# A hybrid decoder step on one core: the input projection split into two passes over the tokens

## The chip, the cores and the metric

The program runs on one core of one Trainium2 chip. Its engines are TensorE (PE; its weight loads are PEld), VectorE (DVE), ScalarE (ACT), GpSimd (POOL) and SyncE (SP), which issues the DMAs. Each engine works through its own instructions in a fixed order and waits on semaphores for the others. The metric is the device time of one execution in microseconds (us).

## The reference

One layer is computed for a prompt group of 2048 tokens and a sample group of 8 x 8 tokens, with the same weights, a model width of 1024 and an inner width of 512 for each of two head groups. In shape:

```
h  = rmsnorm(x);  z = h @ w_in          # 1024 -> 512 | 512 | 4 | 4 | 512 | 512
a_x, a_o, a_i, a_f, b_u, b_g = split(z) # mLSTM input, output gate, gates; GLU value, gate
a_c = silu(causal_conv4(a_x))           # q, k from a_c; v from a_x; 4 heads of 128
ha  = sigmoid(a_o) * headnorm(mlstm_chunkwise(q, k, v, a_i, a_f))   # chunks of 128
u   = b_u * sigmoid(b_g)
cb  = silu(layernorm(causal_conv31(u)))
x   = x + concat(ha, cb) @ w_out
x   = x + cross_attention(rmsnorm(x), memory of 256 tokens) @ x_wo
x   = x + convffn(rmsnorm(x));   y = rmsnorm(x)
```

The mLSTM keeps a 128 x 128 state per head, which goes from chunk to chunk; its decays come from a running sum and a running maximum of the gates. All states are outputs too.

## The kernel before

Every float32 matrix is split into a high part in the matmul format float32r and a low part, and a product is made of three matmuls (`mm3`, line 150): high x high, high x low, low x high. `split` (line 292) makes the high part on ScalarE and the low part on VectorE or GpSimd. The small products of the mLSTM and the transposes are plain float32.

Tokens are worked in 8 chunks of 256 (`CH`); chunk 0 also carries the 64 sample tokens, so its matmuls have 320 columns.

*Input projection* (loop after line 590). For each chunk, `input_part` loads two x tiles, normalises them and makes h, transposed and split, in the tile `ha` or `hb`. Then four parts multiply it by four 512-column pieces of w_in, each held in SBUF as 8 split tiles (32 in all, pool `wp1`): `ogate_part` (weights `wo_`, result to DRAM as `to`), `ax_part` (weights `wa`, the mLSTM's input, to DRAM as `ax`), and `glu_part` (weights `wgt` and `wbv`, result u to DRAM). `gates_part` and `gates_tm_part` make the 8 gate columns with the small weights `wg`. After chunks 3 and 7 `decays` turns the gates of 8 mLSTM tiles into decay factors: a chain of small products in PSUM bank C (`tri`, `av`, `cmo`, `last`, `Mx`), with doubling maximum steps on VectorE between them. The chunk's transposes use banks B and C.

*Depthwise convolution of width 31* (`CONV_BLOCKS`, `conv_block`). It runs over blocks of 1, 2, 2, 2 and 1 chunks, and over the sample group. For each of four channel groups one tap starts the sum in PSUM bank G, most taps are VectorE instructions `psG<-ue,vc,psG`, and the third number of a block, `g` = 10, says how many taps ScalarE multiplies (`cprod`) and GpSimd sums (`cside`) instead. `cvo` is the sum of both; layer norm and swish follow.

*mLSTM loop* (from line 1229). `conv_part` reads `ax` back from DRAM (`axe`) and makes the four-tap convolution `acc`; `qkv_part` makes q and k, `pre_part` the decay matrix `dm`, the decayed q `qi`, v and the weighted k, `recur_part` the recurrence on the state `stt_t`, `head_tail` and `head_out` the head norm and the output gate; the result goes to DRAM as `cat`. Between these, `steps` moves two side programs on: the sample group's mLSTM, and `memory_kv`, the projection of the memory tokens (tiles `hm`). `out_part(t)` reads tile t of `cat` (`ct` is its split form), multiplies it by w_out in banks D and F and adds x: VectorE's `xt<-xt,psD` and `xt<-xt,psF`.

The source gives priorities: the program builder lists each engine's instructions with a timeline of its own and puts, of those that are ready there, the one that comes first in the source. So an engine's order is fixed before the run, and pieces of source that stand apart are interleaved.

Of the kernel before, what the change touches and what calls it, by code (L numbers as in the profile page):

```python
# [9 lines left out]
F32 = mybir.dt.float32  # L10
# [9 lines left out]
P = 128  # L20
# [18 lines left out]
FOLD_AT = 1  # L39
# [54 lines left out]
def trunk_kernel(ctx: ExitStack, tc: tile.TileContext, i: dict, o: list):  # L94
# [67 lines left out]
    xtp = phs.enter_context(tc.tile_pool(name="x1", bufs=2, reuse_waits="tile"))  # L162
# [141 lines left out]
    ax_d = [dram(f"ax{c}", [P, H, CH]) for c in range(NCH)]  # L304
# [11 lines left out]
    wp1 = wa1.enter_context(tc.tile_pool(name="wp1", bufs=32, side="right", reuse_waits="tile"))  # L316
# [44 lines left out]
    def ogate_part(ch, xts, h, n):  # L361
        pts = [mmps() for _ in range(H)]
        if ch == 0:
            for k in range(KT):
                for c in range(H):
                    gemm_k(pts[c], wo_, c * P, h, n, k)
        for c, pt in enumerate(pts):
            if ch:
                gemm_fm(pt, wo_, c * P, h, n)
            tg = ut.tile([P, CH + S], F32, name="tg", tag="tg")  # L370
            act(tg[:, :n], pt[:, :n], AF.Tanh, scale=0.5)
            ts(tg[:, :n], tg[:, :n], 1.0, ALU.add, hnh[:, c:c + 1], ALU.mult)
            for j, (_, nt) in enumerate(xts):
                SY.dma_start(to_d[2 * ch + j if nt == P else NT][:, c, :], tg[:, j * P:j * P + nt])
    def ax_part(ch, xts, h, n):
        for c in range(H):
            pt = mmps()
            gemm_fm(pt, wa, c * P, h, n)
            ax = ut.tile([P, CH + S], F32, name="ax", tag="hu")
            A.copy(ax[:, :CH], pt[:, :CH])  # L380
            SY.dma_start(ax_d[ch][:, c, :], ax[:, :CH])
            if ch == 0:
                A.copy(axs[:, c, :, 3:], pt[:, CH:n].rearrange("p (b t) -> p b t", b=NB))
# [29 lines left out]
    def glu_part(ch, xts, h, n):  # L413
        for c in range(H):
            pg = mmps()
            gemm_fm(pg, wgt, c * P, h, n)
# [130 lines left out]
    def input_part(ch):  # L547
# [6 lines left out]
        return ch, xts, h, CH + (S if ch == 0 else 0)  # L554
# [15 lines left out]
    ts(lnh, vc1[:, o0:o0 + 12], 0.5, ALU.mult)  # L570
    hnh = lnh[:, 8:12]

    wa = load_in(0)
    wgt = load_in(1032 + DA)
    wbv = load_in(1032)
    raws.close()
# [1291 lines left out]
```

## Time and profile before

| | |
|---|---|
| median of 3 runs | 2974.38 us (2971.86 to 2977.52) |
| profiled execution | 2972.23 us, its span 2970.5 us |
| busy in the span | PE 2805.6, PEld 2480.1, DVE 2192.5, ACT 1524.4, POOL 1065.5 us |
| mean granted TensorE clock | 0.969 |
| DMA | 445.63 MB, 150 GB/s on the mean |

Matmuls are pipelined, so the duration of one is longer than the step from one to the next, and a busy PE is not PE at its peak. The change touches what lies before the attention, the first 931 us of the span. A timeline row gives the start, the duration, the engine, the line, the operation, the result and its operands, and, in brackets, how long the engine had been idle and on whom it waited.

### The profile page before, as it was taken

What the parts mean: (1) busy time and instruction counts of PE and PEld (TensorE: products, weight loads), DVE (VectorE), ACT (ScalarE), POOL (GpSimd) and SP (SyncE); (2) the same over time, 40 slices, a digit from 0 to 9 for tenths busy, and PEclk for the clock granted to TensorE, in tenths of its full rate; (3) what the DMA queues carried; (4) which work ended last, traced back from release to release, by engine and by line L of the source; (5) the groups of instructions that cost most, each with busy time, mean ns of one, the idle gap of its engine ahead of it and who ended that gap; (6) DMA issues with size and microseconds to landing.
All of it is one profiled execution on the core that took longest, in us unless ns stands there. A gap on an engine that the chain in (4) does not pass through costs nothing.

```text
span 2970.5 us, 49324 instructions
## 1 busy us (share of the span) xinstructions
PE 2805.6 (94%) x17924; PEld 2480.1 (83%) x17924; DVE 2192.5 (74%) x4066; ACT 1524.4 (51%) x3075; POOL 1065.5 (36%) x1248
## 2 busy tenths in 40 slices
PE   7997997889999799899899999999999999999998
PEld 6996997668887688666588988999989999899987
DVE  3478798986534788745598889877797768877776
ACT  4465665765533665512464446655466545544433
POOL 2235555642210532633433325333253222522222
PEclk9998998979999899999899999999999999999999
DMA  8221223544346422656855555655465545544432
GB/s 193 56 72 50 69 77 124 177 127 158 135 167 218 154 78 96 215 206 228 269 170 163 168 169 195 190 162 161 143 222 160 156 135 164 184 130 133 131 118 75
DMA packets 316571, 445.63 MB, mean 150 GB/s; under 512 B 36605, under 2 KB 219363, under 8 KB 316320
## 3 DMA queue, kind: packets, MB, share of 16 engines
q1 hardware_dynamic: 316328, 442.49, 46.4%
q8 instruction: 141, 2.31, 0.3%
q14 instruction: 102, 0.84, 0.1%
HBM read 348.62 MB, written 94.15 MB: 149 GB/s over the span
## 4 chain that ended last, share of the span: by engine, by line
PE 74%; DVE 13%; DMA 7%; issue 2%; ACT 2%; POOL 1%; SPq 1%; DVEq 0%; POOLq 0%; ACTq 0%
PE psA L148 23%; PE psD L148 14%; PE psF L148 14%; PE psE L148 9%; PE psG L148 8%; DVE psG L122 2%; DMA raw<-in_f_wup 2%; DVE wt L125 2%; PE psC L145 1%; PE psB L145 1%; DVE raw L125 1%; PE psB L148 1%; DVE u L125 1%; DVE acc L122 1%; DMA raw<-in_w_in 1%
## 5 line engine op out<-in xcount | busy, mean ns | idle before, releaser
L294 ACT CAST wt<-raw 128x512 fp32r<-128x512 f32 x888 | 539.5, 620 | 520.5 <-PE psA L148 152.9
L125 DVE TENSOR_TENSOR wt<-raw,wt 128x512 fp32r<-128x512 f32 x666 | 514.5, 788 | 85.3 <-ACT wt L294 81.7
L125 POOL TENSOR_TENSOR wt<-raw,wt 128x512 fp32r<-128x512 f32 x222 | 319.8, 1444 | 671.1 <-ACT wt L294 552.1
L148 PE MATMUL psA<-R,wt 128*128 128x256 f32 (+1 forms) x2448 | 335.4, 287 | 4.6 <-DVE R L122 1.6
L148 PEld LDWEIGHTS psA<-R,wt 128*128 128x128 f32 x2448 | 315.1, 191 | 8.5 <-DVE u L125 1.9
L122 DVE SCALAR_TENSOR_TENSOR psG<-ue,vc,psG 128x512 f32<-128x512 f32 (+2 forms) x488 | 282.5, 579 | 31.3 <-ACT psG L117 22.0
L125 POOL TENSOR_TENSOR cside<-cside,cprod 128x512 f32<-128x512 f32 (+2 forms) x208 | 208.8, 1004 | 140.5 <-ACT cprod L117 86.8
L148 PE MATMUL psA<-wt,ht 128*128 128x512 f32 (+1 forms) x768 | 191.0, 395 | 0.0
L148 PE MATMUL psD<-R,wt 128*128 128x256 f32 (+1 forms) x1248 | 176.6, 286 | 6.9 <-DVE R L125 3.1
L148 PE MATMUL psF<-R,wt 128*128 128x256 f32 (+1 forms) x1248 | 178.2, 287 | 4.3 <-DVE R L122 1.7
L148 PE MATMUL psE<-R,wt 128*128 128x256 f32 (+1 forms) x1224 | 174.4, 287 | 6.2 <-DVE R L125 3.2
L148 PE MATMUL psG<-R,wt 128*128 128x256 f32 (+1 forms) x1224 | 174.7, 287 | 1.9 <-DVE R L122 1.4
L148 PEld LDWEIGHTS psD<-R,wt 128*128 128x128 f32 x1248 | 162.2, 189 | 10.5 <-DVE R L125 4.2
L148 PEld LDWEIGHTS psA<-wt,ht 128*128 128x128 f32 (+1 forms) x768 | 140.6, 185 | 35.0 <-DVE u L125 0.3
L148 PEld LDWEIGHTS psE<-R,wt 128*128 128x128 f32 x1224 | 159.9, 190 | 9.6 <-DVE R L125 4.4
L148 PEld LDWEIGHTS psF<-R,wt 128*128 128x128 f32 x1248 | 162.5, 190 | 6.4 <-DVE u L125 2.4
L148 PEld LDWEIGHTS psG<-R,wt 128*128 128x128 f32 x1224 | 159.8, 190 | 3.1 <-DVE R L122 1.6
L122 DVE SCALAR_TENSOR_TENSOR y<-fe,vc,y 128x512 f32<-128x512 f32 x176 | 130.4, 778 | 14.3 <-ACT y L117 14.3
L117 ACT ACTIVATE cprod<-ue,vc 128x512 f32<-128x512 f32 (+2 forms) x208 | 121.1, 596 | 36.4 <-POOL cside L125 32.6
L148 PE MATMUL psA<-wf,l 128*128 128x512 f32 x516 | 130.9, 401 | 9.0 <-DVE u L125 5.8
L125 POOL TENSOR_TENSOR y<-y,u 128x256 f32<-128x256 f32 x110 | 96.9, 889 | 109.1 <-DVE u L125 90.8
L148 PEld LDWEIGHTS psA<-wf,l 128*128 128x128 f32 x516 | 96.6, 191 | 36.8 <-issue 13.2
(605 smaller groups left out, 6077.4 us busy)
## 6 DMA issues: line engine op xcount, KB each, us to landing
raw<-sum SPq DMA_DIRECT2D x132, 512.0 KB
raw<-in_f_wup SPq DMA_DIRECT2D x110, 512.0 KB
raw<-in_f_wdown SPq DMA_DIRECT2D x88, 512.0 KB
xt<-x SPq DMA_DIRECT2D x48, 512.0 KB
sum<-raw SPq DMA_DIRECT2D x44, 512.0 KB
raw<-in_f_wup SPq DMA_DIRECT2D x66, 256.0 KB
xt<-in_x_prompt SPq DMA_DIRECT2D x32, 512.0 KB
x<-xt SPq DMA_DIRECT2D x32, 512.0 KB
```

Of the source, the lines that this page charges most:

```text
L117: A.activation(out, in_, func, bias=bias, scale=scale)
L122: V.scalar_tensor_tensor(out=out, in0=in0, scalar=s, in1=in1, op0=op0, op1=op1)
L125: (eng or V).tensor_tensor(out=out, in0=a, in1=b, op=op)
L145: T.transpose(out, in_, ident[:n, :n])
L148: T.matmul(out, lhsT, rhs, start=start, stop=stop)
L294: A.copy(hi, src)
```

## The change

The input projection is done in two passes. The first pass makes the gates and the GLU of all chunks, with 16 weight tiles in place of 32, and stores h, split, in DRAM (`h_d`, two stores for a chunk). The weights of the mLSTM's input and of the output gate are loaded while it runs (`load_late`), half of them, and the rest behind it. In the mLSTM loop `rest_part` takes the place of `conv_part`: it loads h of a chunk from DRAM in 8 tiles (a ring of 10), multiplies it by `wa` and by `wo_` in banks D and F, makes the four-tap convolution from the first and the output gate from the second. The buffer `ax` in DRAM goes.

Three more edits go with it. Of the convolution blocks only the first two and the sample's stand ahead of the loop, the others in its iterations 1, 3 and 5 (`CONV_AT`), and ScalarE and GpSimd take 12 taps, not 10. `decays` is called after the next chunk's `input_part`. The side programs move on from iteration 7 only, and the output projections, which were spread over the loop from its third iteration, come in its last iteration and behind it.

```diff
-CONV_BLOCKS = [(0, 1, 10), (1, 2, 10), (3, 2, 10), (5, 2, 10), (7, 1, 10)]
+CONV_BLOCKS = [(0, 1, 12), (1, 2, 12), (3, 2, 12), (5, 2, 12), (7, 1, 12)]
+W2_EARLY = 4
+H2_BUFS = 10
+CONV_AT = {1: 2, 3: 3, 5: 4}
...
-    xtp = phs.enter_context(tc.tile_pool(name="x1", bufs=2, reuse_waits="tile"))
+    xtp = xw = ctx.enter_context(tc.tile_pool(name="xw", bufs=6, side="right", reuse_waits="tile"))
...
-    ax_d = [dram(f"ax{c}", [P, H, CH]) for c in range(NCH)]
+    h_d = [dram(f"h{c}", [P, KT, 2, CH + (0 if c else S)]) for c in range(NCH)]
...
-    wp1 = wa1.enter_context(tc.tile_pool(name="wp1", bufs=32, side="right", reuse_waits="tile"))
+    wp2 = wa2.enter_context(tc.tile_pool(name="wp2", bufs=KT + W2_EARLY, side="right", reuse_waits="tile"))
+    wp1 = wa1.enter_context(tc.tile_pool(name="wp1", bufs=2 * KT, side="right", reuse_waits="tile"))
...
+    def load_late(pool, c0, k):
+        raw = xw.tile([P, 2, 512], F32, name="raw", tag="xt")
+        SY.dma_start(raw, w_in[k * P:(k + 2) * P, c0:c0 + DA].rearrange("(z p) c -> p z c", p=P))
+        out = []
+        for z in range(2):
+            w = pool.tile([P, 2, 512], F32R, name="wt", tag="wt")
+            split(w[:, 0], w[:, 1], raw[:, z], eng=(V, G)[z])
+            out.append([w])
+        return out
...
+        n = CH + (S if ch == 0 else 0)
+        for z in range(2):
+            SY.dma_start(h_d[ch][:, :, z], f(h[:, z, :, :n]))
...
     for ch in range(NCH):
-        order = (ogate_part, ax_part, gates_part, None, glu_part, gates_tm_part)
+        cur_ = cur
+        gates_part(*cur)
         if ch:
-            order = (gates_part, glu_part, gates_tm_part, None, ogate_part, ax_part)
...
+            glu_part(*cur)
+            gates_tm_part(*cur)
+        if ch + 1 < NCH:
+            cur = input_part(ch + 1)
         if ch == 0:
+            glu_part(*cur_)
+            gates_tm_part(*cur_)
             fold_qk()
-        cur = nxt
+        elif len(late) > (KT - W2_EARLY) // 2:
+            late_part(wp2)
+        if 2 * ch + 2 in (GB, NT):
+            decays(2 * ch + 2 - GB)
...
-    def conv_part(ch):
+    def rest_part(ch):
+        n = CH + (S if ch == 0 else 0)
+        hs = []
+        for k in range(KT):
+            hk = h2p.tile([P, 2, CH + S], F32R, name="h2", tag="h2")
+            SY.dma_start(f(hk[:, :, :n]), h_d[ch][:, k])
+            hs.append(hk)
+        def gemm(wts, c):
+            pt = mmps()
+            for k in range(KT):
+                w, m = wts[k][0], slice(c * P, c * P + P)
+                mm3(pt[:, :n], (w[:, 0, m], w[:, 1, m]), (hs[k][:, 0, :n], hs[k][:, 1, :n]), k == 0, k == KT - 1)
+            return pt
         t = m1.tile([P, H, 3 + CH], F32, name="axe", tag="axe")
-        SY.dma_start(t[:, :, 3:], ax_d[ch])
...
+        for c in range(H):
+            pt = gemm(wa, c)
+            A.copy(t[:, c, 3:], pt[:, :CH])
...
         conv4(acc, lambda c, j: t[:, c, j:j + CH])
         st_[ch] = acc
+        for c in range(H):
+            pt = gemm(wo_, c)
+            tg = ut2.tile([P, CH + S], F32, name="tg", tag="tg")
+            act(tg[:, :n], pt[:, :n], AF.Tanh, scale=0.5)
+            ts(tg[:, :n], tg[:, :n], 1.0, ALU.add, hnh[:, c:c + 1], ALU.mult)
+            for j in range(2):
+                SY.dma_start(to_d[2 * ch + j][:, c, :], tg[:, j * P:j * P + P])
...
     for ch in range(NCH + 2):
         if ch < NCH:
             qkv_part(ch)
         if ch + 1 < NCH:
-            conv_part(ch + 1)
+            rest_part(ch + 1)
+        if ch == NCH - 1:
+            wa2.close()
+            wpo0 = out_pool("wpo0", 0, WO_FIRST)
+            next(fold)
+            wout = load_out(wpo0, 0, WO_FIRST)
...
-            if ch > 2:
-                out_part(2 * ch - 6 + j)
...
+            if ch == NCH + 1:
+                for _ in range(2):
+                    out_part(outs.pop(0))
...
+        if ch in CONV_AT:
+            conv_block(*CONV_BLOCKS[CONV_AT[ch]])
+    while outs:
+        out_part(outs.pop(0))
+        steps(0)
```

Three places show how the order moves. The line numbers of the helpers differ by 3 between the programs. The first is TensorE at the first decay chain, at the end of chunk 3. Before (`hb,wt` is chunk 3's projection, `ha` chunk 4's, `ident,cvo` a transpose of the convolution):

```order
L145 MATMUL psC<-ident,av 32x128
L148 MATMUL psD<-hb,wt 128x256 x5
L148 MATMUL psF<-hb,wt 128x256 x24
L145 MATMUL psC<-ident,cmo 128x32
L148 MATMUL psC<-Fs,last 128x32
L148 MATMUL psC<-Mx,last 128x32
L145 MATMUL psE<-ident,cvo 128x128
L145 MATMUL psC<-ident,Mx 32x128
L145 MATMUL psC<-ident,xt 128x128 x2
```

Now, the same chain (its later products follow in the same manner):

```order
L151 MATMUL psC<-wk,tri 128x32
L148 MATMUL psB<-ident,xt 128x128 x2
L151 MATMUL psA<-ha,wg 8x256
L151 MATMUL psA<-ha,wg 16x256
L151 MATMUL psA<-ha,wg 8x256
L151 MATMUL psA<-ha,wt 128x256 x5
L151 MATMUL psD<-ha,wt 128x256 x5
L151 MATMUL psF<-ha,wt 128x256 x5
L148 MATMUL psC<-ident,av 32x128
L151 MATMUL psA<-ha,wt 128x256
```

Before, four products of the chain follow each other and chunk 4's transposes stand behind them; now chunk 4's projection lies between them.

The second is TensorE at the start of the mLSTM loop. Before (`acc,wqk` makes q and k of chunk 0, `stt_t,qi` is the first product of the recurrence):

```order
L148 MATMUL psF<-hb,wt 128x256 x24
L148 MATMUL psA<-acc,wqk 128x256 x4
L148 MATMUL psC<-wk,tri 128x32
L145 MATMUL psE<-ident,cvo 128x128
L145 MATMUL psC<-ident,av 32x128
L148 MATMUL psA<-wqkv,axe 128x128 x4
L148 MATMUL psA<-qk,acc 128x128 x4
L145 MATMUL psA<-ident,acc 128x128 x4
L148 MATMUL psB<-stt_t,qi 128x129
```

Now, some rows behind the first product of the recurrence (`h_...` are tiles of h read back from DRAM):

```order
L148 MATMUL psA<-ident,acc 128x128 x3
L151 MATMUL psA<-wqkv,axe 128x128 x3
L148 MATMUL psE<-ident,cvo 128x128
L151 MATMUL psA<-wqkv,axe 128x128
L151 MATMUL psD<-h_4686,wt 128x256 x3
L148 MATMUL psC<-ident,Mx 32x128
L151 MATMUL psD<-h_4688,wt 128x256 x3
L151 MATMUL psD<-h_4690,wt 128x256 x3
L151 MATMUL psB<-vv,dm 128x129
L151 MATMUL psF<-h_4686,wt 128x256
```

Before, the loop's first chunk has only its own small products; now deferred projection products lie between them and the second decay chain's.

The third is VectorE in a later chunk of the mLSTM loop. Before (`stt_t` is the state's update, `acc` the four-tap convolution):

```order
L122 SCALAR_TENSOR_TENSOR stt_t<-stt_t,ex,psC 128x129
L122 SCALAR_TENSOR_TENSOR acc<-axe,vc_383,acc 128x256 x3
L122 SCALAR_TENSOR_TENSOR acc<-th,acc 128x512 x2
L125 TENSOR_TENSOR xt<-xt,psD 128x512
L125 TENSOR_TENSOR to<-to,psA 128x512
L122 SCALAR_TENSOR_TENSOR stt_t<-stt_t,ex,psC 128x129 x2
L122 SCALAR_TENSOR_TENSOR dm<-mr,av,cap 128x128 x4
L125 TENSOR_TENSOR qi<-qi,qk 128x512
L125 TENSOR_TENSOR xt<-xt,psF 128x512
```

Now:

```order
L125 SCALAR_TENSOR_TENSOR psG<-ue,vc_394,psG 128x512
L714 RECIPROCAL hw<-hw 128x8
L125 SCALAR_TENSOR_TENSOR psG<-ue,vc_394,psG 128x512 x2
L125 SCALAR_TENSOR_TENSOR stt_t<-stt_t,ex,psC 128x129
L125 SCALAR_TENSOR_TENSOR psG<-ue,vc_394,psG 128x512
L125 SCALAR_TENSOR_TENSOR acc<-axe,vc_388,acc 128x256
L125 SCALAR_TENSOR_TENSOR psG<-ue,vc_394,psG 128x512
L125 SCALAR_TENSOR_TENSOR acc<-axe,vc_388,acc 128x256 x3
```

Before, the additions of the output projection stand between the mLSTM's operations; now taps of the long convolution do.

## Rows read from the trace of the kernel before

**Rows 1.** Stages: window, length, busy (instructions) PE, PEld, DVE, ACT, POOL, clock, DMA share, GB/s

```profile
0.00:100.00 100.00, 77.93 (x467) 72.31 (x468) 38.57 (x83) 42.93 (x90) 22.14 (x36) 0.95 0.68 159
100.00:250.00 150.00, 147.45 (x1224) 144.31 (x1223) 103.04 (x262) 90.15 (x205) 66.22 (x100) 1.00 0.21 61
250.00:290.00 40.00, 21.13 (x152) 19.02 (x151) 37.46 (x69) 18.11 (x32) 25.64 (x31) 0.74 0.13 39
290.00:490.00 200.00, 199.40 (x1665) 196.94 (x1662) 164.34 (x292) 125.42 (x253) 97.45 (x113) 1.00 0.24 75
490.00:690.00 200.00, 160.57 (x794) 125.20 (x795) 179.85 (x417) 137.48 (x337) 110.92 (x129) 0.80 0.50 159
690.00:931.00 241.00, 236.10 (x1294) 199.35 (x1291) 104.35 (x220) 96.08 (x270) 34.88 (x47) 1.00 0.42 146
```

**Rows 2.** Three tiles: ns min/median/max, first to last start in us, forms

```profile
L122 DVE SCALAR_TENSOR_TENSOR psG<-ue,vc,psG x488: 270/490/757, 82.9 to 693.6; 128x512 f32<-128x512 f32 x80, 128x256 f32<-128x256 f32 x54, 128x64 f32<-128x64 f32 x29
L125 DVE TENSOR_TENSOR xt<-xt,psD x17: 678/686/689, 690.5 to 952.3; 128x512 f32<-128x512 f32 x16, 64x512 f32<-64x512 f32 x1
L148 PE MATMUL psA<-wt,mT x42: 387/389/501, 931.3 to 967.8; 128*128 128x512 f32 x42
```

**Rows 3.** Timeline of PE at the first decay chain, rows with a wait

```profile
266.28 0.31 PE L145 MATMUL psC<-ident,cmo 32*128 32x32 f32 x1 [8.51 <-DVE cmo L125]
267.04 0.64 PE L148 MATMUL psC<-Fs,last 128*128 128x32 f32 x2 [0.45 <-DVE Mx L526]
...
271.63 0.47 PE L145 MATMUL psE<-ident,cvo 128*128 128x128 f32 x1 [3.52 <-DVE cvo L125]
277.18 0.40 PE L145 MATMUL psC<-ident,Mx 128*32 128x128 f32 x1 [5.08 <-POOL Mx L125]
```

**Rows 4.** Timeline of PE at the start of the mLSTM loop, two waits

```profile
507.37 0.80 PE L148 MATMUL psB<-stt_t,qi 128*128 128x129 f32 x2 [9.87 <-DVE qi L125]
...
515.42 2.08 PE L148 MATMUL psA<-wqkv,axe 128*128 128x128 f32 x8 [2.77 <-DVE dm L125]
```

**Rows 5.** Waits of DVE at 490 to 700, the longest: us, times, longest

```profile
DVE stt_t L122 <- PE psC L148: 8.4, 4, 3.7
```

**Rows 6.** Paces of PE: two pieces of the chain, two timeline rows (start, us)

```profile
117.21 2.88 PE psD L148 x24
...
904.01 5.52 PE psD L148 x24
...
716.14 0.39 PE L148 MATMUL psB<-stt_t,qi 128*128 128x129 f32 x2
716.36 0.39 PE L148 MATMUL psB<-vv,dm 128*128 128x129 f32 x2
```

**Rows 7.** Groups by form at 0 to 940: busy us, mean ns, idle before

```profile
L122 DVE SCALAR_TENSOR_TENSOR psG<-ue,vc,psG 128x512 f32<-128x512 f32 x240 | 179.7, 749 | 7.8 <-ACT psG L117 3.9 <-DMA ue<-u 0.6
L122 DVE SCALAR_TENSOR_TENSOR psG<-ue,vc,psG 128x256 f32<-128x256 f32 x160 | 77.5, 484 | 15.9 <-ACT psG L117 12.9
L117 ACT ACTIVATE cprod<-ue,vc 128x512 f32<-128x512 f32 x108 | 76.5, 720 | 22.8 <-POOL cside L125 20.8 <-DMA ue<-u 1.7
L125 POOL TENSOR_TENSOR cside<-cside,cprod 128x512 f32<-128x512 f32 x108 | 142.9, 1323 | 63.3 <-ACT cprod L117 52.0 <-DVE psG L122 5.8
```

**Rows 8.** The decay matrix's mask at 430 to 700, then at 700 to 930

```profile
L122 DVE SCALAR_TENSOR_TENSOR dm<-mr,av,cap 128x128 f32<-128x128 f32 x32 | 14.2, 497 | 0.2 <-PE psB L148 0.2
...
L122 DVE SCALAR_TENSOR_TENSOR dm<-mr,av,cap 128x128 f32<-128x128 f32 x32 | 9.1, 346 | 7.4 <-PE psB L148 7.3
```

**Rows 9.** DMA issues of weights at 0 to 950

```profile
raw<-in_w_in SPq DMA_DIRECT2D x32, 256.0 KB
...
raw<-in_w_out SPq DMA_DIRECT2D x16, 256.0 KB
raw<-in_x_wk SPq DMA_DIRECT2D x16, 256.0 KB
```

**Rows 10.** The costliest group of projection products at 0 to 940

```profile
L148 PE MATMUL psA<-hb,wt 128*128 128x256 f32 x768 | 99.1, 285 | 0.5 <-ACT tg L117 0.5
```

More of the change, by code (lines that the diff above doesn't have):

```diff
@@ L413, in glu_part @@
     def glu_part(ch, xts, h, n):
-        for c in range(H):
-            pg = mmps()
-            gemm_fm(pg, wgt, c * P, h, n)
+        if ch == 0:
+            pgs = [mmps() for _ in range(H)]
+            for k in range(KT):
+                for c in range(H):
+                    gemm_k(pgs[c], wgt, c * P, h, n, k)
+        for c in range(H):
+            if ch == 0:
+                pg = pgs[c]
+            else:
+                pg = mmps()
+                gemm_fm(pg, wgt, c * P, h, n)
             tg = ut.tile([P, CH + S], F32, name="tg", tag="tg")
@@ L578, in trunk_kernel, with late_part @@
     first_loads()
+    wa, wo_ = [], []
+    late = [(wl, c0, k) for wl, c0 in ((wa, 0), (wo_, DA)) for k in range(0, KT, 2)]
+    def late_part(pool):
+        wl, c0, k = late.pop(0)
+        wl.extend(load_late(pool, c0, k))
     for ch in range(NCH):
[L580 removed]
+        cur_ = cur
+        gates_part(*cur)
         if ch:
[L582 to L589 removed]
+            glu_part(*cur)
+            gates_tm_part(*cur)
+        if ch + 1 < NCH:
+            cur = input_part(ch + 1)
         if ch == 0:
+            glu_part(*cur_)
+            gates_tm_part(*cur_)
             fold_qk()
[L592 removed]
+        elif len(late) > (KT - W2_EARLY) // 2:
+            late_part(wp2)
+        if 2 * ch + 2 in (GB, NT):
+            decays(2 * ch + 2 - GB)
     wa1.close()
@@ L1184, in conv_part @@
         st_[ch] = acc
+        for c in range(H):
+            pt = gemm(wo_, c)
[4 more added lines that the diff above has]
+                SY.dma_start(to_d[2 * ch + j][:, c, :], tg[:, j * P:j * P + P])
+            if ch == 0:
+                SY.dma_start(to_d[NT][:, c, :], tg[:, CH:n])
     mrs = {}
@@ L1227, in steps @@
             next(fold, None)
-    wpo0 = out_pool("wpo0", 0, WO_FIRST)
-    conv_part(0)
-    next(fold)
-    wout = load_out(wpo0, 0, WO_FIRST)
+    rest_part(0)
+    outs = list(range(NT - 2))
     for ch in range(NCH + 2):
@@ L1240, in trunk_kernel @@
                 recur_part(ch - 1, j)
+            if ch >= NCH - 1:
                 steps(0)
@@ L1262, in trunk_kernel @@
             head_tail(m2, nds[ch - 1], P, 2, ex[:, 0, 2 * ch - 2:2 * ch])
+        if ch in CONV_AT:
[3 more added lines that the diff above has]
+        steps(0)
+    for _ in side:
+        pass
+    ahead = [out_load(t) for t in (NT, NT - 2)]
+    out_part(NT, ahead[0])
     for _ in side:
```

70 lines of the change are left out of this document (20 added, 50 removed).

## The prediction, made before the run

> **What bounds the kernel now.** I read the table by stages first, then the instructions that mark the stages' ends, then the waits inside them. The stages [rows 1]: to 490 us the input projection, with the depthwise convolution beside it; 490 to 690 the mLSTM loop with the rest of the convolution and the memory projection; 690 to 931 the output projection beside the rest of the mLSTM. The reader is to see that the limit changes. From 100 to 250 and from 290 to 490 TensorE is full (147.5 of 150, 199.4 of 200 us) and VectorE has room (103.0 and 164.3, or 82% in the second). From 490 to 690 it is turned round: VectorE is busy 179.9 of 200 us. From 690 to 931 TensorE is full again and VectorE is busy 104.4 of 241 us. The markers are the first convolution tap at 82.9, the first addition of an output projection at 690.5 and the first product of the attention's value factors at 931.3 [rows 2]. What comes after that last marker is the same work in the same order in both programs, so I forecast when it starts and carry the difference to the end.
>
> Between these stages TensorE stands still for reasons of order. At 250 to 290 it is busy 21.1 of 40 us: the decay chain on VectorE must come through, and TensorE's next projection work stands behind the chain's small products; it waits 8.5, 0.5, 3.5 and 5.1 us, 17.6 together [rows 3]. At the mLSTM's start it waits 9.9 and 2.8 us, with nothing else in its queue that could run [rows 4]. In the VectorE-bound stage the longest sum of named waits of VectorE is 8.4 us [rows 5]: it is its own work that fills it.
>
> **The change part by part.** Paces: 24 products of 256 columns take 2.88 us, 0.12 each; 24 of 512 columns 5.52 us, 0.23 each; a float32 product of 128 columns 0.22 (716.14 to 716.36) [rows 6].
>
> Start. Each weight matrix has 8 tiles of 256 KB; four of them (32 issues [rows 9]) are loaded before the loop now, two then. Chunk 0 first ran the output gate and the mLSTM input, 2 x 4 x 24 products of 320 columns, at 0.12 x 320/256 = 0.15 each 28.8 us, before it came to the GLU. Those leave, so the first tap comes about 26 us sooner, at 57 (the loads set a floor: 159 GB/s went through in the first 100 us [rows 1], and 4.2 MB fewer have to).
>
> TensorE. No product is added or removed. What it needs ahead of the output projections becomes 2688 x 0.12 + 384 x 0.15 + 128 gate products x 0.12 = 396; 192 of the memory projection x 0.23 = 44; 336 float32 products x 0.22 and 32 of twice the width x 0.44 = 88; and about 500 transposes at 0.11, with the sample group some 70: 600 us, an estimate from the order's counts and the paces. The output projections, 768 products x 0.23 = 177 us, now stand alone behind it, where before the rest of the mLSTM lay beside them. The stalls of [rows 3] go, because the decay products now lie between projection products; those of [rows 4] go, because chunk 0's and 1's deferred products lie there.
>
> VectorE. Up to 690 us it was busy 38.6 + 103.0 + 37.5 + 164.3 + 179.9 = 523.3 us [rows 1]. Of the 104.4 us of the next stage, 30 residual additions at 0.686 (20.6) [rows 2] and 6 operand splits of twice their width (at most 2 x 0.686 each, 8) stay with the output projections; the other 76 now come ahead of them. Two taps per tile go to ScalarE and GpSimd: 12 tiles x 2 x 0.749 + 8 x 2 x 0.484 = 25.7 us less [rows 7]. The masks of the decay matrix took 0.497 us while GpSimd summed taps and 0.346 later [rows 8]; 32 of them now lie beside taps, 4.8, with the convolution of four taps 6 us more. Sum: 523.3 + 76 - 25.7 + 6 = 580, of which about 20 fall before the first tap (half of the first 100 us). 560 us remain. A rule of the Trainium skill bears on this (page "SBUF — State Buffer", section "SBUF: two separate sides"): VectorE and GpSimd hold a shared port exclusively, VectorE when it has two SBUF inputs. [Rows 8] agree in direction; by the rule every such operation pays, and at the row's 0.15 for the 32 masks and 36 four-tap steps that is 10 us in place of 6. It speaks against moving taps to GpSimd, and changes the sum by 4.
>
> What hides the rest. GpSimd gets 24 x 1.323 and 16 x about 0.8, 44 us more; ScalarE 24 x 0.72 and 16 x 0.5, 25 us more [rows 7]; in 490 to 690 they were busy 55% and 69% [rows 1], so nothing is charged. If this cover fails, it is the rival below. The rows h go to DRAM (17 MB) and come back (17 MB, 64 issues on SP's queue), the 8.4 MB of the old intermediate go. The DMA share was 0.24 at 290 to 490 and 0.50 at 490 to 690 [rows 1]; 17 MB over 280 us are 61 GB/s beside 75. Not shown by the trace is how TensorE meets h's return: eight of ten buffers are held until the last product group of a chunk, and eight tiles at 159 GB/s take 13 us. I bound this by 0 (ten buffers and mLSTM products between) and 7 x 10 = 70 us of TensorE time, and take 0, since TensorE has 17% of room in the sum below.
>
> The sum. With a share e of VectorE the first output addition is at 57 + 560/e, and the marker of 931 comes 177 - 3 = 174 us later. e was 0.82 where TensorE was full (290 to 490) and 0.90 where VectorE bound (490 to 690). Both must now run together, so I take 0.84, nearer the lower: 57 + 667 = 724, + 174 = 898, which is 33 us before 931. The profiled execution took 2972.2 us (span 2970.5), 2.2 below the median of the runs; 2972 - 33 = 2939, say 2940. TensorE then works 600 of 707 us from 17 on, 85%. No change is at e = 0.80 (560/0.80 = 700).
>
> **The rivals.** Better overlap: at e = 0.88 the marker is at 867, 64 us sooner, 2908. For it: 290 to 490 has TensorE at 99.7% with VectorE at 82%. Against it: there was no recurrence in it.
>
> The tail eats it: no change. The memory projection, w_out and the sample group's state ran beside the mLSTM before; now they start only when the last deferred rows are done. 48 weight tiles of 256 KB ([rows 9]; the value weights have as many as the key weights), states and stores are about 21 MB; at 159 GB/s 132 us, against the 91 x 0.954/0.84 = 103 us of VectorE work that I count there (estimated from the order and the mean durations). That loses 29 of the 33 us: 2968. Against it: 159 GB/s took only half of the DMA engines' time at 490 to 690 [rows 1].
>
> Two banks: slower. The deferred products have two PSUM banks (D and F) in place of four, each emptied by ScalarE, which now has more taps in front. A group lasts 2.88 us, so a copy that comes over 2.9 us late stops TensorE, and with it the recurrence that VectorE waits for. Up to no change TensorE may stand still 757 - 600 - 17 = 140 us, 2.2 us for each of 64 groups: a copy 5 us late, seven products of 0.72 [rows 7]. At 3 us a group it starts the output projections at 809 and the marker is at 983, 52 us later: 3024. With four banks TensorE waited 0.5 us in the costliest projection group [rows 10], which speaks against it; ScalarE's 69% for it. A rule of the Trainium skill (page "Perfetto Trace Analysis", section "Matmul Optimizations") asks for all eight banks to be used; no run here shows two at this pace.
>
> That rows are not deferred, or the loop not filled, is excluded by the order.
>
> **How the numbers follow.** About 0.2%, 6 us, is what can be told from no change; that is e from 0.79 to 0.81. Forecast, e 0.82 to 0.87: 0.45. Better overlap: 0.13. Tail: 0.17, of which 0.07 within 6 us and 0.10 still faster. Slower by banks, late h tiles or a stiff order (e under 0.79): 0.25. Faster 0.68, same 0.07, slower 0.25. The range goes from e = 0.90 (marker at 853, 78 sooner, 2894) to e = 0.77 (958, 27 later, 2999): 2895 to 3000.
>
> **What would show it.** First tap near 57; no TensorE wait of over 3 us at the two decay chains; in the loop both engines above 80%, the granted clock near 1.00 where it was 0.80; first output addition near 724; then 5.5 us per product group of 24 without waits; first product of the value factors near 898. Wrong would be waits of TensorE on ScalarE's copies from banks D and F, on h tiles, or a stretch between the last deferred product and the first output projection of over 130 us.

## The result, and the profile after

The changed kernel takes 3011.89 us (median of 4 runs, 3008.20 to 3012.39), the kernel before in the same session 2975.61: ratio 1.0121, 95% interval 1.0103 to 1.0138. It is slower by 36 us, where 33 faster was forecast. The profiled execution took 3008.2 us (span 3006.2).

The stages after, with the columns of [rows 1]: start, first pass, loop with the deferred products, the stretch behind the last of them, output projections up to the first value-factor product.

```profile
0.00:100.00 100.00, 52.37 (x281) 42.97 (x282) 31.50 (x68) 32.13 (x66) 19.59 (x34) 0.83 0.73 185
100.00:343.00 243.00, 213.04 (x1635) 200.37 (x1634) 182.75 (x410) 169.45 (x357) 147.51 (x190) 0.94 0.38 122
343.00:649.00 306.00, 283.07 (x2221) 274.43 (x2221) 277.18 (x535) 212.14 (x545) 145.15 (x180) 0.98 0.36 111
649.00:794.50 145.50, 132.79 (x691) 103.67 (x691) 87.24 (x230) 89.45 (x229) 69.62 (x94) 0.88 0.64 201
794.50:965.50 171.00, 169.29 (x765) 136.84 (x763) 35.84 (x55) 18.95 (x30) 20.13 (x9) 1.00 0.40 136
```

The markers of [rows 2] after:

```profile
L125 DVE SCALAR_TENSOR_TENSOR psG<-ue,vc,psG x448: 267/490/824, 70.6 to 695.9; 128x512 f32<-128x512 f32 x72, 128x256 f32<-128x256 f32 x48, 128x64 f32<-128x64 f32 x30
...
L128 DVE TENSOR_TENSOR xt<-xt,psD x24: 674/689/690, 794.5 to 1486.7; 128x512 f32<-128x512 f32 x23, 64x512 f32<-64x512 f32 x1
...
L151 PE MATMUL psA<-wt,mT x42: 387/389/775, 965.5 to 1003.5; 128*128 128x512 f32 x42
```

The last marker moved from 931.3 to 965.5: 34 of the 36 us are lost ahead of it. In the first 100 us TensorE worked 52.4 us, against 77.9 before. The first pass has it at 88%, the loop at 93% with VectorE at 91%; behind the last deferred product VectorE falls to 60%.

The mean granted clock of the first 100 us was 0.83, against 0.95 before. What took the start is seen on three engines. The timeline of TensorE, two rows with their wait:

```profile
85.89 5.23 PE L151 MATMUL psD<-ha,wt 128*128 128x320 f32 x24 [11.09 <-ACT tg L120]
...
97.78 3.78 PE L151 MATMUL psF<-ha,wt 128*128 128x320 f32 x24 [2.88 <-ACT tg L120]
```

The timeline of ScalarE at the tanh that TensorE waits for:

```profile
85.40 0.44 ACT L120 ACTIVATE tg<-psD 128x320 f32<-128x320 f32 x1 [5.52 <-DMA out<-ot]
97.30 0.44 ACT L120 ACTIVATE tg<-psF 128x320 f32<-128x320 f32 x1 [5.70 <-DMA out<-ot]
```

The issues of SyncE's queue just before:

```profile
74.53 1.26 SPq L557 DMA_DIRECT2D h<-hb  x2
75.84 4.02 SPq L435 DMA_DIRECT2D out<-ot  x1
```

The tanh's tile `tg` and the small tile `ot` (the sample's convolution state, stored from chunk 0's GLU) share one tag with two buffers: a ring, whose buffers the tiles take in turn. The store of `ot` was issued right behind two h stores of 1024 KB; until it landed, the tanh had no buffer, the tanh held the PSUM bank, and TensorE stood. To 120 us ScalarE waited 16.1 us for `out<-ot`; before, when the GLU came third and no h was stored, 4.1 us to 200 us.

The decay chain, which answers to [rows 3], on TensorE's timeline after (rows with a wait at 240 to 246):

```profile
241.38 0.69 PE L148 MATMUL psB<-ident,xt 128*128 128x128 f32 x2 [4.19 <-DVE hb L125]
243.80 0.39 PE L148 MATMUL psC<-ident,gT 16*128 16x16 f32 x2 [1.52 <-DVE cmo L545]
245.42 0.66 PE L148 MATMUL psC<-ident,xt 128*128 128x128 f32 x2 [1.23 <-DVE gall L128]
```

The waits for the chain's own results fell from 14.0 us (the 17.6 of [rows 3] hold 3.5 for the convolution's `cvo`) to 1.5; instead TensorE waits beside it for the input of the next chunk (`hb`), 4.2 us at the longest. And TensorE's waits at 343 to 694, which answer to [rows 4]: total, times, longest.

```profile
PE psC L151 <- DVE stt_t L125: 11.8, 6, 6.5
PE psD L151 <- DMA h<-h: 5.4, 5, 2.3
...
PE psD L151 <- ACT axe L1211: 1.9, 2, 1.0
...
PE psF L151 <- DMA h<-h: 1.6, 2, 1.1
```

### The profile page after: what moved, and what is told of

It is laid out like the page before. It is cut to its first block, busy times and chain, and to the rows that moved or that the text cites. A ratio compares the mean times of both kernels' runs of the same rounds, so it can differ in the third digit from the quotient of the medians.

```text
span 3006.2 us, 49437 instructions
## 1 busy us (share of the span) xinstructions
PE 2815.6 (94%) x17924; PEld 2483.7 (83%) x17924; DVE 2179.5 (72%) x4022; ACT 1536.3 (51%) x3115; POOL 1115.3 (37%) x1299
## 4 chain that ended last, share of the span: by engine, by line
PE 70%; DVE 14%; DMA 8%; issue 3%; ACT 2%; POOL 2%; SPq 1%; DVEq 0%; POOLq 0%; ACTq 0%
PE psA L151 20%; PE psD L151 15%; PE psF L151 14%; PE psE L151 9%; PE psG L151 9%; DVE psG L125 3%; DMA raw<-in_f_wup 2%; DVE wt L128 2%; DMA raw<-in_w_in 1%; PE psB L148 1%; PE psC L148 1%; DMA h<-h 1%; DVE acc L125 1%; DVE raw L128 1%; DVE dm L125 1%
## 5 line engine op out<-in xcount | busy, mean ns | idle before, releaser
L128 POOL TENSOR_TENSOR cside<-cside,cprod 128x512 f32<-128x512 f32 (+2 forms) x248 | 251.5, 1015 | 137.5 <-ACT cprod L120 94.4
L125 DVE SCALAR_TENSOR_TENSOR psG<-ue,vc,psG 128x512 f32<-128x512 f32 (+2 forms) x448 | 256.9, 573 | 13.3 <-ACT psG L120 5.6
L120 ACT ACTIVATE cprod<-ue,vc 128x512 f32<-128x512 f32 (+2 forms) x248 | 146.3, 603 | 32.0 <-POOL cside L128 30.9
```

The costliest lines, as they stand in the source:

```text
L120: A.activation(out, in_, func, bias=bias, scale=scale)
L125: V.scalar_tensor_tensor(out=out, in0=in0, scalar=s, in1=in1, op0=op0, op1=op1)
L128: (eng or V).tensor_tensor(out=out, in0=a, in1=b, op=op)
```

## The experiments

All but the first two rows were timed in five rounds beside the kernel before. Medians are compared; the ratio is to the kernel before, with its 95% interval. Kernels of different sessions meet in these comparisons, and the median of the kernel before went from 2972.9 to 2975.6 us between sessions, so differences under 3 us say nothing. "Marker" is the first value-factor product, "busy" TensorE's busy time up to it, by the same view of each profiled execution, "idle" the difference.

| kernel | us | ratio | marker | busy | idle |
|---|---|---|---|---|---|
| before | 2975.6 | 1 | 931.3 | 842.6 | 88.7 |
| after | 3011.9 | 1.0121 (1.0103 to 1.0138) | 965.5 | 850.6 | 114.9 |
| own_ot | 2979.2 | 1.0019 (1.0007 to 1.0030) | 935.6 | 845.4 | 90.2 |
| h_act | 3003.9 | 1.0092 (1.0077 to 1.0108) | 964.5 | 852.9 | 111.6 |
| h_not_stored | 3002.6 | 1.0089 (1.0074 to 1.0104) | 964.3 | 856.8 | 107.5 |
| close_early | 3021.6 | 1.0152 (1.0136 to 1.0167) | 974.1 | 853.1 | 121.0 |
| before_ot | 2964.6 | 0.9968 (0.9958 to 0.9978) | 920.0 | 838.5 | 81.5 |
| h_act_ot | 2994.1 | 1.0056 (1.0036 to 1.0076) | 950.4 | 852.9 | 97.5 |
| mem_first | 3019.0 | 1.0150 (1.0131 to 1.0170) | 979.3 | 874.0 | 105.3 |
| taps10_ot | 2978.9 | 1.0011 (1.0000 to 1.0021) | 933.1 | 850.4 | 82.7 |
| wout_v | 2979.1 | 1.0013 (1.0002 to 1.0024) | 934.6 | 848.0 | 86.6 |
| mem1_after | 2957.2 | 0.9945 (0.9928 to 0.9962) | 914.4 | 824.2 | 90.2 |
| mem1_before | 2941.4 | 0.9888 (0.9871 to 0.9905) | 896.9 | 807.0 | 89.9 |
| before_decays_ot | 2955.9 | 0.9938 (0.9920 to 0.9955) | 917.6 | 845.2 | 72.4 |
| before_best | 2959.7 | 0.9952 (0.9940 to 0.9964) | 919.3 | 846.0 | 73.3 |
| own_rings | 2983.2 | 1.0036 (1.0024 to 1.0048) | 943.9 | 852.0 | 91.9 |
| hp_input | 2985.6 | 1.0045 (1.0033 to 1.0057) | 944.9 | 851.9 | 93.0 |
| nost_ot | 2981.3 | 1.0032 (1.0020 to 1.0045) | 936.8 | 850.9 | 85.9 |
| pe_first | 2987.5 | 1.0046 (1.0028 to 1.0063) | 951.4 | 868.7 | 82.7 |
| pe_loop | 3005.7 | 1.0104 (1.0088 to 1.0121) | 961.0 | 871.4 | 89.6 |

**The start.** Four kernels from the changed one: the ring, the queue, the stores, and (against them) the tail.

```
own_ot:        -  ot = ut.tile([S, P], F32, name="ot", tag="tg")
               +  ot = ut.tile([S, P], F32, name="ot", tag="ot")
h_act:         -  SY.dma_start(h_d[ch][:, :, z], ...)
               +  A.dma_start(h_d[ch][:, :, z], ...)
h_not_stored:  +  if ch == 0:            # around the stores; rest_part reads h_d[0]
close_early:   -  if ch == NCH - 1: wa2.close() ...   steps from ch >= NCH - 1
               +  if ch == NCH - 2: wa2.close() ...   steps from ch >= NCH - 2
```

own_ot. 

> The tile ot (rows of the sample's convolution state) gets buffers of its own and no longer takes turns with the tanh's tile tg. Theory 'ring': ScalarE's tanh waited 16.1 us for the stores of ot before 120 us and 6.6 us later, and PE 11.1 + 2.9 us for that tanh: these waits go, 8 to 15 us off 3011.9. Rival: ScalarE then waits for the late weights or x instead and the time stays within 4 us.

h_act. 

> The h stores are issued from ScalarE's queue and no longer from SyncE's; nothing else changes. Theory 'start' in the form 'order in the queue': weights, x tiles and the stores of ot no longer stand behind 2 x 1280 and 2 x 1024 KB; first convolution tap nearer the forecast 57 us than the 70.6 seen, PE idle in 50 to 100 us 33 -> about 15 us, 10 to 25 us off 3011.9. Rival 'bytes, not order': the transfers share the same engines and take as long from either queue: within 5 us of 3011.9, first tap at 70 again.

h_not_stored. 

> Only chunk 0's h is stored, and the deferred products of all eight chunks read that one back, so the gates of chunks 1 to 7 are computed from wrong rows; the reading, the products and everything behind them stay. Theory 'start': the h stores stand in the one transfer queue ahead of weights, x tiles and small stores. But chunk 0's own store (2 x 1280 KB, issued at 25.0 us) stays here, so only what chunk 1's store (issued at 74.5) and the later ones cost can go: the wait of the tanh for the store of ot and the late x of chunk 1, 10 to 25 us off the changed kernel's 3011.9, most of it before 130 us. Rival 'late weights': the start is lost to ScalarE's casts of the late weights, whoever is in the queue: under 5 us. Neither expects the tail behind 650 us to move.

close_early. 

> The pool of the deferred weights is closed one step of the loop earlier (right behind the products of the last chunk), and the memory projection and the sample group start there, at step 6 and no longer at step 7. Theory 'tail': these two are exposed behind 650 us because nothing else is left to run beside them; one step of the loop earlier they find some 40 us of work beside them, 20 to 40 us off 3011.9, all of it between the last deferred product (648.7) and the first product with value factors (965.5). Rival 'full loop': VectorE is about 90% busy in the loop, so what is moved there lengthens it by as much: within 8 us of 3011.9.

The ring was the larger cost by far: own_ot takes 33 us off, more than twice what was expected. The stall had pushed all of the first pass back: without it its last product comes at 296.5 and no longer at 339.9. The stages of own_ot, columns as above:

```profile
0.00:100.00 100.00, 76.79 (x482) 68.17 (x483) 36.39 (x82) 43.02 (x89) 23.86 (x41) 0.93 0.72 194
100.00:299.00 199.00, 179.43 (x1414) 168.35 (x1412) 158.60 (x372) 143.55 (x310) 127.33 (x163) 0.97 0.43 143
299.00:608.00 309.00, 280.77 (x2215) 273.81 (x2216) 277.82 (x526) 214.47 (x543) 152.76 (x188) 0.98 0.35 110
608.00:762.20 154.20, 137.43 (x708) 107.62 (x708) 105.07 (x262) 98.68 (x253) 83.12 (x107) 0.87 0.59 190
762.20:935.60 173.40, 171.01 (x774) 137.67 (x772) 36.17 (x56) 19.99 (x34) 20.13 (x9) 1.00 0.39 138
```

The reader is to see the first row: 76.8 us of TensorE, as before, in place of 52.4, at a granted clock of 0.93 in place of 0.83. The first tap came at 67.5 us there (DVE's first row on psG), still 10 behind the forecast 57. h_act (8 us) and h_not_stored (9) fall between their expectations (under 5, or 10 to 25 us): with the stores on ScalarE's queue the tanh still waited 11.5 us for `out<-ot`. So the stores seem to cost what they cost mainly by delaying a small store in whose ring an engine waits; nost_ot, below, bears this out.

close_early is slower by 10, against its theory. Its products of the memory projection start 16 us sooner and the output projections 13 us later than after (791.1 against 778.1); at 640 to 676 its TensorE worked half the time:

```profile
640.00:676.00 36.00, 18.34 (x110) 14.95 (x109) 35.28 (x85) 25.25 (x64) 23.66 (x48) 0.71 0.55 167
676.00:748.00 72.00, 72.00 (x385) 58.19 (x385) 38.21 (x99) 45.59 (x115) 28.55 (x32) 0.96 0.54 174
748.00:800.00 52.00, 49.02 (x224) 35.49 (x223) 23.06 (x65) 22.46 (x67) 18.34 (x16) 0.77 0.64 209
```

**Ring mended: what is left.** Is the ring the change's doing, and what do queue, tail and VectorE cost once it is gone? All but the first start from own_ot.

```
before_ot:  the kernel before, with the edit of own_ot
h_act_ot:   own_ot with the edit of h_act
mem_first:  own_ot;  conv_block(*CONV_BLOCKS[1])
         +  for _ in memory_kv():      # moved here from the loop's end
         +      pass
taps10_ot:  own_ot;  CONV_BLOCKS: third number 12 -> 10
wout_v:     own_ot;  load_out: eng=G -> eng=V
```

before_ot. 

> The kernel before, with buffers of its own for ot, and nothing of the change. If the wait of the tanh for the stores of ot is the change's own doing (the GLU, with its ot, now comes first, while the h stores and late loads stand in the queue), this does little here: the tanh waited 4.1 us for them before 200 us, so 0 to 4 us off 2974.4. Rival 'the ring was a fault of both kernels, and the change is faster without it': 20 to 33 us off here too, about 2945 to 2955.

h_act_ot. 

> The changed kernel with buffers of its own for ot, and the h stores issued from ScalarE's queue. If the order in SyncE's queue costs something beside the ring (first tap 66.9 with the ring mended, forecast 57), 5 to 12 us off the 2979.2 of the one with ot alone. If the two were one cost, seen from two sides, 0 to 3 us.

mem_first. 

> Ring mended as before, and the whole memory projection moved from behind the last deferred rows to the end of the first pass, where its pool fits into the space of the first pass's weights. Theory 'tail': 154 us lay between the last deferred product (607.6) and the first output addition (762.2) with VectorE at about half; 192 products of 0.23 us, 44 us, leave that stage and run beside the convolution of blocks 0 and 1, where VectorE is the busier: first output addition 20 to 40 us sooner, 20 to 40 us off 2979.2. Rival 'nothing gained by place': the first stage and the loop have TensorE at 90% themselves, so they grow by 44 us less their 10% of room: within 8 us of 2979.2.

taps10_ot. 

> Ring mended as before, and the taps that ScalarE and GpSimd take over back at 10 per tile from 12, so 25.7 us of taps return to VectorE. If VectorE's work still sets the end of the loop (share 0.90 from 200 to 650 us), 15 to 28 us more than 2979.2. If TensorE's order or the tail sets it, or if the taps on GpSimd slow VectorE's own work: within 8 us.

wout_v. 

> Ring mended, and the splits of the output projection's weights on VectorE and no longer on GpSimd. In the changed kernel these 32 tiles come when VectorE is idle (9.0 of 32 us busy at 730 to 762) and take GpSimd 1.3 us each, with SyncE waiting 26.7 us for them to free the two raw buffers. If w_out's loading is what the tail ends on, 6 to 15 us off 2979.2; if TensorE (29.1 of 32 us busy there) or its clock (0.73) is, within 4 us.

The kernel before gains 10 us by the same edit, between its two expectations: a third of the ring's price was there already, the rest is the change's. With the ring mended in both, the changed kernel is still 14.6 us slower (2979.2 against 2964.6): of the 36 us, the ring accounts for 22 and the rest of the change for about 15.

h_act_ot is a miss: 15 us slower than own_ot. The products of rows h in bank D, with their first and last start, own_ot and then h_act_ot:

```profile
L151 PE MATMUL psD<-h,wt x768: 274/283/562, 299.6 to 604.3; 128*128 128x256 f32 x168, 128*128 128x320 f32 x24
```

```profile
L151 PE MATMUL psD<-h,wt x768: 274/283/615, 314.1 to 620.1; 128*128 128x256 f32 x168, 128*128 128x320 f32 x24
```

The loss is there before any row h is read back: 14.5 us at the first deferred product, 14.8 at the marker. TensorE then waited 13.6 us for rows h, against 5.0 in own_ot, but the loss did not grow with it. At 150 to 250 it worked 81.0 us, against 89.2; why the first pass is longer is open. wout_v changes nothing, so GpSimd's splits of w_out don't end the tail.

taps10_ot is the first blow to the forecast's premise. 25.7 us of taps (by the forecast's rows) went back to VectorE, whose busy time up to the marker rose by 12.8; the time did not change. Up to the marker, own_ot and then taps10_ot:

```profile
0.00:935.60 935.60, 845.44 (x5587) 755.62 (x5587) 614.05 (x1296) 519.70 (x1226) 407.20 (x506) 0.96 0.46 144
```

```profile
0.00:933.10 933.10, 850.35 (x5586) 758.73 (x5586) 626.89 (x1335) 497.55 (x1186) 364.06 (x466) 0.96 0.46 144
```

The edit also takes 22.2 us of work off ScalarE and 43.1 off GpSimd, so it does not test VectorE alone. By stages two effects cancel: the first deferred product comes 7.7 us later (307.3), the last 2.6 us sooner (605.0), so the deferred products take 10 us less. What is shown is that the exchange of taps was worth nothing in sum.

mem_first is 40 us slower, and shows both halves of the trade: the stretch behind the last deferred product fell from 154 to 107 us as expected, but where the projection now stands TensorE worked 62 of 96 us and the first deferred product came 97 us later (396.5 against 299.6):

```profile
300.00:396.00 96.00, 62.48 (x248) 45.82 (x248) 82.50 (x140) 65.90 (x122) 67.84 (x75) 0.81 0.53 172
396.00:689.00 293.00, 279.44 (x2199) 272.87 (x2200) 248.40 (x489) 202.42 (x526) 127.50 (x159) 0.98 0.35 109
689.00:796.00 107.00, 94.84 (x458) 74.92 (x457) 56.33 (x164) 49.50 (x152) 37.85 (x62) 0.70 0.43 133
```

**Is the tail exposed?** The same cut in both kernels, ring mended in both, and the one part of the change that looked like a gain, alone:

```
mem1_after, mem1_before:  memory_kv
    -  for k in range(KT):          -  ... k == 0, k == KT - 1)
    +  for k in range(1):           +  ... k == 0, k == 0)
before_decays_ot:  before_ot, decays(...) moved from behind gates_tm_part
    to the end of the chunk's turn, behind input_part of the next
```

mem1_after. 

> The changed kernel with the ring of ot mended, and of the memory projection only the first of eight steps of the sum over k: 168 of 192 products (at 0.23 us 39 us of TensorE), 28 of 32 weight tiles and their splits are left out, so the memory's keys and values are wrong. Theory 'tail': in the changed kernel this work stands alone between the deferred rows and the output projections, so its time goes whole: of the 76 us that it took there (653.8 to 729.8) 50 to 70 off 2979.2. Rival 'the time is TensorE's work wherever it stands': about 39 us, as much as in the kernel before.

mem1_before. 

> The same left out of the kernel before with the ring mended (168 of 192 products of the memory projection, 28 of 32 weight tiles and splits). Theory 'tail': there it lay beside the mLSTM, whose pace VectorE set (busy 179.9 of 200 us), and its TensorE work filled idle time; 28 splits on VectorE and GpSimd and some of the products go: 10 to 30 us off 2964.6, at least 25 us less than the same edit takes off the changed kernel. Rival: 39 us or more, as much as there.

before_decays_ot. 

> The kernel before with the ring mended and, of the change, only the place of the decay chains: behind the next chunk's input and not ahead of it. The waits of TensorE in the first chain (8.5, 0.5, 3.5 and 5.1 us) should go, as they did in the changed kernel: 10 to 18 us off 2964.6 if TensorE sets the time there (250 to 290 it worked 21 of 40 us). Rival: VectorE had 37.5 of those 40 us of work, and the taps that wait for it are late instead: within 5 us.

The cut takes 22 us off the changed kernel and 23 off the kernel before; both are under the 38.6 us that the products take at their pace, so the rival of "as much as TensorE's work" missed too. The theory that the tail's work is dearer in the changed kernel falls: the stretch is long, but its work costs no more there than beside the mLSTM. The decay chains' place is worth 9 us alone (8.7 of medians), about half of the 17.6 us of waits. The stretch of the first chain, before_ot and then before_decays_ot:

```profile
250.00:300.00 50.00, 31.22 (x229) 28.81 (x230) 44.49 (x78) 24.15 (x42) 25.35 (x33) 0.76 0.14 45
```

```profile
250.00:300.00 50.00, 48.99 (x409) 48.06 (x409) 46.47 (x86) 30.24 (x58) 33.73 (x39) 1.00 0.15 47
```

TensorE's idle time there fell from 18.8 to 1.0 us, but up to the marker only from 81.5 to 72.4: half of it came back later. This kernel, 0.9938 of before, has the lowest time of all that compute the whole output, and is faster than both kernels.

**Where the given-back time went.** With the ring mended, three guesses at it, and the best of before with one more buffer:

```
own_rings:   own_ot;  gT: tag="tg" -> tag="gT", bufs=1
hp_input:    own_ot;  + with tc.high_priority():  around cur = input_part(ch + 1)
nost_ot:     own_ot with the edit of h_not_stored
before_best: before_decays_ot with the edit of own_rings
```

own_rings. 

> Buffers of their own for ot and also for the gates' tile gT, which otherwise holds one of the tanh's two buffers from the start of a chunk to its end. Theory 'ring, second part': TensorE waited 2.4 + 2.4 + 1.9 us for ScalarE's copy of gT at 100 to 200 us, and such waits in each of eight chunks sum to 10 to 15 us; 6 to 15 us off the 2979.2 of the kernel with ot alone mended. Rival: the copy of gT is late because ScalarE's queue is full (0.6 to 0.8 busy): within 4 us.

hp_input. 

> Ring of ot mended, and the input part of chunks 1 to 7 (norm, transposes, operand splits) put ahead of the taps in the order of every engine. Theory 'short first pass': a chunk has only 8 product groups (23 us) now, and the next chunk's input on ScalarE and VectorE is late; TensorE's idle 27 us at 100 to 350 fall to about 12: 8 to 18 us off 2979.2. Rival: the input was early enough, and taps that are put off end later: within 5 us, or up to 10 more.

nost_ot. 

> Ring of ot mended, and the h of chunks 1 to 7 not stored; the deferred products of all chunks read chunk 0's rows, so the gates of chunks 1 to 7 are computed from wrong rows. The price of 14 MB of stores without the ring: if they crowd the transfer queue, 8 to 15 us off 2979.2 (9 with the ring as it was); if the ring was how they cost, under 3 us.

before_best. 

> The kernel before with buffers of their own for ot and gT, and the decay chains behind the next chunk's input. Before 200 us TensorE is full there, so gT's buffer should matter little: 2950 to 2956, as much as with ot and the decay chains alone (2955.9). If gT's share of the ring costs time in every chunk, whatever the order, 2940 to 2948.

All three guesses fail: none is faster (4, 6 and 2 us slower by the medians, of which only hp_input's interval lies clear of own_ot's). The 14 MB of stores cost nothing that can be seen without the ring; gT's buffer and the input's place are not the reason; before_best is level with before_decays_ot.

**Which engine sets the time.** The last two add work to TensorE and to nobody else:

```
pe_first:  own_ot, glu_part, ch > 0      pe_loop:  own_ot, rest_part, ch > 0
   +  for _ in range(2 if c == 0 else 1):   +  for k in [*range(KT)] * (2 if wts is wa
          gemm_fm(pg, wgt, c * P, h, n)            and c == 0 and ch else 1):
```

pe_first. 

> Ring of ot mended, and in the first pass one product group of the GLU per chunk computed twice over in the same place (chunks 1 to 7, 7 x 24 products of 0.12 us, 20.2 us of TensorE added, nothing for any other engine). If TensorE sets the time there: 13 to 20 us more than 2979.2. If the forecast's room of 15% is there, or VectorE or the transfers set it: under 6 us more.

pe_loop. 

> The same for one deferred group per chunk in the loop (chunks 1 to 7, again 20.2 us of TensorE added beside the mLSTM, nothing for any other engine). If TensorE sets the time of the loop: 13 to 20 us more than 2979.2. If VectorE (0.90 busy there) sets it, as the forecast had it: under 6 us more.

pe_loop is 26.5 us slower for 20.2 us of products. Up to the marker, and from 299 us to its last deferred product:

```profile
0.00:961.00 961.00, 871.44 (x5755) 781.29 (x5755) 609.99 (x1296) 521.17 (x1226) 405.74 (x506) 0.95 0.44 140
299.00:624.80 325.80, 306.49 (x2391) 299.18 (x2391) 286.67 (x546) 224.03 (x562) 163.59 (x200) 0.97 0.33 105
```

TensorE's busy time rose by 26.0 us and the marker by 25.4, but not all of it in the loop. The last deferred product came 17.2 us later (624.8), with 19.3 us of idle time in that stage in place of 28.2. The other 8 us came behind the first output addition, where nothing was added (182.9 us to the marker in place of 173.4); why is open. So most of the added work lengthens the loop, although VectorE is at 0.88 to 0.90 in that stage. The added group also stands ahead of the copy `axe`, which the four-tap convolution waits for; the two were not tested apart.

pe_first costs 8 us by the medians, between the two expectations; its six runs spread from 2984.8 to 2997.9, and the profiled one is the longest. Its first pass behind 100 us:

```profile
100.00:324.00 224.00, 202.83 (x1603) 191.93 (x1601) 176.55 (x399) 158.33 (x336) 144.48 (x184) 0.95 0.40 130
```

In that execution the first pass took none of the products into its idle time (21.2 us, against 19.6): the first deferred product came 24.8 us later, at 324.4. At the marker 15.8 us were left, so 9 were regained behind the first pass.

## Why the prediction was wrong

The failed step is the sum: "With a share e of VectorE the first output addition is at 57 + 560/e", with e = 0.84, in which TensorE has 600 us to do and is busy "85%". VectorE's work was sized rightly (580 us up to the first output addition; 578.7 measured, the sum of the first four stages), but its share was not reached. From the first tap to the first output addition, after and then own_ot:

```profile
70.60:794.50 723.90, 641.93 (x4614) 589.74 (x4614) 558.83 (x1199) 475.94 (x1141) 364.05 (x465) 0.94 0.43 135
```

```profile
67.50:762.20 694.70, 626.63 (x4554) 577.04 (x4554) 557.85 (x1199) 471.57 (x1136) 369.04 (x465) 0.95 0.44 140
```

The share was 0.77, and 0.80 with the ring mended, the value at which the forecast itself puts no change. TensorE was busy 90% of the second stretch, so it had less room than the forecast gave it. Its need was the term that was mis-sized: put at 600 us from counts and paces, its busy time up to the first output addition was 681.3 (the same four stages). Part of the difference can be the clock: the paces of [rows 6] stand in stages with a granted clock of 1.00 ([rows 1]), and the four stages had 0.83, 0.94, 0.98 and 0.88; how much that makes was not separated from products that were not counted. The rows held a warning: [rows 1] sum to 842.6 us of TensorE up to the marker, where the forecast has 600 + 177, and the products stay the same. Every version of the same 5586 or 5587 matrix instructions but mem_first is busy 838 to 857 us there. A marker at 898 therefore asked for idle time of 55 us in place of 89, of which the first 100 us alone had 22. What an "e" hid is this: the exchange of taps in taps10_ot was worth nothing, while of 20.2 us of added products 17.2 reached the end of the loop in pe_loop.

Seen as idle time, the change did what it should and gave it back. With the ring mended, the kernel before (before_ot):

```profile
0.00:100.00 100.00, 80.81 (x519) 75.11 (x520) 40.77 (x92) 48.86 (x101) 23.12 (x38) 0.97 0.66 165
100.00:250.00 150.00, 147.58 (x1236) 145.82 (x1234) 110.09 (x271) 92.11 (x208) 73.89 (x106) 1.00 0.21 63
...
300.00:450.00 150.00, 150.00 (x1263) 148.47 (x1263) 122.44 (x213) 97.58 (x197) 71.97 (x70) 1.00 0.24 74
450.00:550.00 100.00, 71.11 (x443) 61.63 (x442) 97.44 (x194) 61.27 (x132) 62.18 (x88) 0.85 0.43 137
550.00:920.00 370.00, 357.81 (x1906) 293.93 (x1904) 211.40 (x495) 186.89 (x509) 99.54 (x123) 0.94 0.45 151
```

It is idle 19 us in its first 100, 2 to 250, 19 at 250 to 300, none at 300 to 450, 29 at 450 to 550, 12 after: two lumps, and stretches where TensorE is full. The changed kernel (own_ot) is idle 23 in the first 100, then 20 in the first pass, 28 in the loop, 17 behind it, 2 after: no lump, and no full stretch ahead of the output projections. That is 90.2 us in place of 81.5, and its busy time is 6.9 us longer. To reach 898, the lumps had to go and the projection work had to stay as full as it was alone ([rows 1], 0.3% idle at 290 to 490); mixed with chains of small dependent steps it is 9% idle. The largest sum of waits is the one for the state, at 350 to 640 in own_ot:

```profile
PE psC L151 <- DVE stt_t L125: 16.0, 8, 4.4
```

Why the rest was given back is open: three edits that should have shortened it did not.

Point by point:
- First tap 57: 70.6, and 67.5 without the ring. The forecast took the products off the time of the first tap and named the loads as a floor, without a time; what holds the tap at 67.5 was not tested. A shared tag was overlooked, which cost the changed kernel 33 us and the one before 10.
- Decay stalls gone: right for the chain's own results, 1.5 us left. By the sign that was named (no wait over 3 us at the chains) it failed, with 4.2 us for `hb`. And the place was worth 9 us, not 17.6: idle time came back elsewhere.
- Start of the mLSTM: the waits of [rows 4] for `qi` and `dm` went but for 1.2 us. Those for `stt_t` grew: 6.2 us from 490 to 931 before, 11.8 from 343 to 694 after.
- Both engines over 80% in the loop, clock near 1.00: right (93% and 91%, 0.98).
- h traffic, "hidden": right once the ring is mended, no gain without the stores (nost_ot); in the ring they cost. The return made 7.0 us of waits, near the lower bound taken.
- Extra taps on ScalarE and GpSimd, "nothing is charged": in sum the exchange bought and cost nothing (taps10_ot), so the 25.7 us that it saves on VectorE were worth nothing, or were paid for elsewhere.
- "Two banks" did not happen: TensorE's products in banks D and F waited 4.4 us for ScalarE in all (2.9 for `axe`, 1.5 for the tanh). The page "Perfetto Trace Analysis" of the Trainium skill (section "Matmul Optimizations"), which asks for all eight banks to be used, did not decide here.
- "The tail eats it": the sign that was named (over 130 us) was just missed by the first output projection, 129.4 us behind the last deferred product at 778.1, and came by the first output addition, 145.8 us behind it. Its reason fell: the cut gains the same in both kernels.
- The page "SBUF — State Buffer" of the Trainium skill (section "SBUF: two separate sides"): the direction agrees in part. The masks `dm` took 0.493 us in the loop beside GpSimd's sums, as in [rows 8]; with 43.1 us less on GpSimd in taps10_ot their mean fell from 0.538 to 0.396 us, 9.2 us of VectorE in all. That is the largest single part of why 25.7 us of taps lengthened VectorE's busy time by only 12.8. But the four-tap steps went the other way, from 0.639 to 0.713. The masks, own_ot and then taps10_ot, up to 933:

```profile
L125 DVE SCALAR_TENSOR_TENSOR dm<-mr,av,cap 128x128 f32<-128x128 f32 x64 | 30.8, 538 | 4.0 <-PE psB L151 4.0
```

```profile
L125 DVE SCALAR_TENSOR_TENSOR dm<-mr,av,cap 128x128 f32<-128x128 f32 x64 | 21.6, 396 | 2.4 <-PE psB L151 2.3
```

The rival that came true in its result, slower, was given 0.25 for other reasons (banks, late h tiles or a stiff order). Its share under 0.79 did come, at 0.77, but with the ring mended it is 0.80. The range ended 12 us below the time.

## What to carry to other kernels

Before a share of one engine is stretched over a program, add up the busy column of every engine over the whole stretch: with 842.6 of 931 us on TensorE, and that sum nearly the same in all versions with the same products, little but its idle time could be won. The question is where it will be idle afterwards, not how much VectorE has left. The product stream that was full when it stood alone did not stay full here when it was mixed with dependent chains, so a lump that is removed should be counted as won only in part. And look at what shares a ring of buffers: a 32 KB store behind 2 MB in the same queue held a bank, then TensorE.

## What the runs showed of the hardware

Work taken from or given to TensorE did not change its busy time by its pace. Leaving out 168 products of 512 columns (0.23 us each, 38.6 us) took 21.3 us off its busy time in the changed kernel and 31.5 in the kernel before, while the mean granted clock up to the marker fell from 0.96 to 0.94 and from 0.94 to 0.93 (both kernels with the ring mended). Adding 168 products of 256 columns (20.2 us) raised it by 23.3 us in the first pass and 26.0 in the loop. Versions with the same products differ by up to 18 us in this busy time, so the 3 to 17 us between these figures and the pace cannot be told from what other edits do.
